# Order of the down passes, a fifth Strassen group and the spacing of the attention heads in a macaron block kernel

## The chip, the cores and the metric

The kernel runs on one core of a Trainium2 chip. The metric is the device time of one launch in microseconds (us), as the median of several runs. TensorE multiplies, VectorE and ScalarE do the elementwise work, GpSimd (POOL) and SyncE issue most of the transfers between HBM and the on-chip memory (SBUF), and TensorE writes its results to eight banks of PSUM.

## What is computed

One block on 256 frames of 2048 channels, all in float32, cut to its products:

```python
x = x + 0.5 * swiglu_ffn(rmsnorm(x), w1_gate, w1_up, w1_down)          # inner width 5632
proj = rmsnorm(x) @ w_in                                              # 2048 -> 11264
q_a, k_a, v_a, q_r, k_r, v_r, g_r, gate_a, gate_r = split(proj)
branch_a = chunked_band_attention(q_a, k_a, v_a, rel_bias) @ w_out_att  # 8 heads of 128
ret = chunkwise_retention(rotary(q_r), rotary(k_r), v_r)              # 8 heads of 128
branch_r = (silu(g_r) * ret) @ w_out_ret
x = x + (sigmoid(gate_a) * branch_a + sigmoid(gate_r) * branch_r) @ w_out
x = x + 0.5 * swiglu_ffn(rmsnorm(x), w2_gate, w2_up, w2_down)
return rmsnorm(x)
```

`swiglu_ffn` is `(silu(h @ gate) * (h @ up)) @ down`.

## The kernel before

**Products.** Every weight element is used once, so the weights stream through the chip (459.50 MB are read). A float32 weight chunk of 256 x 512 is split into a high part (`hi`, cast by ScalarE, L121) and a remainder (`lo`, subtracted by VectorE, L122); the activations are split likewise, and `three` (L129 to L131) makes one product of three matmuls: hi times hi, lo times hi, hi times lo.

**Steps.** The whole program is a list `steps`, numbered from 0 in the order in which they run; in the tile names of the standard steps (`hi587`) the number is that of the step. A *standard* step (`standard`, L133) is one chunk of an ordinary product: 12 matmuls of 512 columns. Two ordinary blocks of 512 output columns can instead be made together by `Strassen` (L479) in 28 steps of 6 matmuls, in four phases: phases 0 to 2 take four pairs of steps each (one step on a loaded quarter of the weights, one on a sum of quarters) and phase 3 takes four steps. The sums cost VectorE more than the split: in phase 0 each pair has one addition beside its two splits (L494), in phase 1 each pair has two (L549 and L536), in phases 2 and 3 there is none.

**Weaving.** `weave` (L634) places standard steps between the pairs of the Strassen groups, at a rate of standard steps per pair that it spreads by the table `SHARE`, heaviest in phase 1. A standard step waits in the queue until the blocks it needs are at hand (`job.needs`, `at_hand`, L645). In both feed-forward stages (`ffn`, L674) two of the eleven blocks (9 and 10, `PLAIN`) are ordinary; the other nine are Strassen groups that pair a block's gate and up. The standard steps are those of the plain blocks and of the passes of down: `PASSES` says which two inner blocks each pass of four column blocks takes.

**Run.** `run` (L220) goes through the steps. At step c it first prepares weights up to step c + 3 (`prep_upto`: ScalarE's cast and VectorE's remainder; there are four buffers, so that the cast of step c + 3 waits until the products of step c - 1 are through), then runs the functions that are due at c (`later`, `at`), then issues the products of step c, and, where a block ends there, its `done`.

**The middle.** First comes the woven part: four Strassen groups of the merge gates and the standard blocks of q, k and v of the attention (steps 372 to 531). Then standard steps alone: v and the gate of the retention (`nat_done` with Silu for the gate), its q and k with the rotation by `cos` and `sin` (`ret_qk_done`, L800, twelve VectorE instructions of 128 x 256), the output products of both branches. Beside these run, as functions that are due at a step, the attention (`attention`, L840: scores, transposes, values, two steps apart; heads four steps apart from eight steps after `mixed`, the first step behind the woven part) and the retention (L897).

**Side banks.** Scores, transposes and values of the heads, and every small transpose (`transpose4`, L345), take a PSUM tile by `side_tile` (L90), of which there are two: a third tile waits until the readers of one of the two before it are done. Each engine works through its instructions in the order in which they are written; nothing is reordered by a planner.

Of the kernel before, what the change touches and what calls it, by code (L numbers as in the profile page):

```python
# [8 lines left out]
F32 = mybir.dt.float32  # L9
F32R = mybir.dt.float32r  # L10
AF = mybir.ActivationFunctionType
# [4 lines left out]
P = 128  # L16
SEQ = 256
NT = SEQ // P
D = 2048
# [7 lines left out]
NB = 512  # L27
# [12 lines left out]
MIX_LEAD = 8  # L40
# [1 line left out]

SHARE = (0.85,) * 4 + (1.0,) * 4 + (0.8,) + (0.4,) * 3 + (0.15,) * 4
PLAIN = (9, 10)
PASSES = ((9, 0), (10, 1), (2, 3), (4, 5), (6,), (7,), (8,))
WARM = (6, 3)
TAIL_PARTS = ((0, slice(0, NB)), (1, slice(0, NB // 2)), (1, slice(NB // 2, NB)))

# [22 lines left out]
def block_kernel(ctx: ExitStack, tc: tile.TileContext, x, g1, w1g, w1u, w1d, gm, w_in, rel, woa, wor, wo,  # L71
                 g2, w2g, w2u, w2d, gf, cos, sin, decay, ident, out):
    nc = tc.nc
# [8 lines left out]
    dram = ctx.enter_context(tc.tile_pool(name="dram", bufs=1, space=bass.MemoryType.DRAM))  # L82

    def act_tile(dt, name):
        return apool.tile([P, 4, SEQ], dt, tag="act", name=name)
# [7 lines left out]
    def tmp_tile(name, tag="t", bufs=None):  # L93
        return tmp.tile([P, NB], F32, tag=tag, name=name, bufs=bufs)
# [9 lines left out]
    def later(n, fn):  # L104
        due.setdefault(state["step"] + n, []).append(fn)
# [87 lines left out]
    def add(jobs):  # L193
        for job in jobs:
            for k in range(0, job.nk, KC):
                steps.append(standard(job, k))
# [558 lines left out]
    nm = Norm("nm", gains[:, 1, :], True)  # L755
# [11 lines left out]
    QA, KA, VA, QR, KR, VR, GR, GA, GG = 0, W, 2 * W, 3 * W, 4 * W, 5 * W, 6 * W, 7 * W, 7 * W + D  # L767
    scale = HD ** -0.5
    tposed, nat = {}, {}
# [56 lines left out]
    def nat_done(key, b, func, after=None):  # L826
        def done(acc):
            dst = act_tile(F32, f"{key}{b}")
            nat[key, b] = dst.rearrange("p a q -> p (a q)").rearrange("p (t n) -> p t n", t=NT)
            for t in range(NT):  # L830
                nc.scalar.activation(nat[key, b][:, t, :], acc[t], func, scale=nm.scale(t))
            if after is not None:
                after()

        return done
# [56 lines left out]
    def all_attention():  # L892
        for h in range(HEADS):
            for s, stage in enumerate(attention(h)):
                later(2 + 4 * h + 2 * s, stage)

    def retention(b):  # L897
        outs = {}
# [53 lines left out]
    def proj(col, done, tags=("acc", "z")):  # L952
        return Gemm(w_in0, 0, col, D // P, nm, done, tags)


    gate_dram = [
        [dram.tile([P, NT, NB], F32, name=f"sig{key}{b}") for key in "ar"] for b in range(D // NB)
    ]

    def merge_gates(b):  # L960
        def evict(t, side, r):
            if side == 1:
                nc.scalar.activation(r, r, AF.Sigmoid)
            else:
                bank, r = r, tmp_tile(f"sg{b}{t}", "gate", 2)
                nc.scalar.activation(r, bank, AF.Sigmoid, scale=nm.scale(t))
            nc.scalar.dma_start(gate_dram[b][side][:, t, :], r)

        return Strassen(nm, w_in0, GA + b * NB, w_in0, GG + b * NB, evict)

    both = ("acc", "acc")
    weave(
        [proj(QA + b * NB, att_qk_done("qa", b), both) for b in range(2)]
        + [proj(KA + b * NB, att_qk_done("ka", b), both) for b in range(2)]
        + [proj(VA + b * NB, nat_done("va", b, AF.Copy), both) for b in range(2)],
        0, {b: (lambda b=b: merge_gates(b)) for b in range(D // NB)}, MIX_LEAD,
    )
    mixed = len(steps)
    add([proj(VR + b * NB, nat_done("vr", b, AF.Copy)) for b in range(2)])
    add([proj(GR + b * NB, nat_done("gr", b, AF.Silu)) for b in range(2)])  # L980
    for b in range(2):
        add([proj(QR + b * NB, ret_qk_done("qr", b)), proj(KR + b * NB, ret_qk_done("kr", b, lambda b=b: retention(b)))])

    merged = Operand("mg", D // NB)
    merges, of_ret = [], []
    for b in range(D // NB):
        sig = {}

        def load_sig(b=b, sig=sig):
            for i, key in enumerate("ar"):  # L990
                t = act_tile(F32, f"sig{key}{b}").rearrange("p a q -> p (a q)")
                sig[key] = t.rearrange("p (t n) -> p t n", t=NT)
                nc.gpsimd.dma_start(sig[key], gate_dram[b][i])

        def branch_a_done(acc, sig=sig):
            for t in range(NT):
                nc.vector.tensor_mul(sig["a"][:, t, :], acc[t], sig["a"][:, t, :])

        def branch_r_done(acc, sig=sig, b=b):
            for t in range(NT):  # L1000
                nc.vector.tensor_mul(sig["r"][:, t, :], acc[t], sig["r"][:, t, :])
                nc.vector.tensor_add(sig["r"][:, t, :], sig["r"][:, t, :], sig["a"][:, t, :])
            later(2, lambda: [merged.put(b, t, sig["r"][:, t, :]) for t in range(NT)])

        merges.append((len(steps), load_sig))
        add([Gemm(woa[0], 0, b * NB, W // P, att, branch_a_done)])
        of_ret.append(Gemm(wor[0], 0, b * NB, W // P, ret, branch_r_done))
# [52 lines left out]
    def at(step, fn):  # L1060
        due.setdefault(step, []).append(fn)
# [52 lines left out]
    at(mixed, set_bias)  # L1114
    at(mixed + 8, all_attention)
    at(mixed + 8, lambda: later(8, load_gain(g2, 2)))
    at(mixed + 20, set_decay)
    for step, fn in merges:
        at(step - 8, fn)
# [64 lines left out]
```

## Time and profile before

| | us |
|---|---|
| median of 3 runs (2104.57 to 2106.90) | 2105.74 |
| the profiled execution | 2106.03 |
| its span, first to last instruction | 2104.1 |
| TensorE busy | 2069.0 (98%) |
| VectorE busy | 1733.5 (82%) |
| ScalarE busy | 1396.6 (66%) |

Times in the rows are microseconds from the start of the span. A timeline row has the start, the duration of one instruction (or of several merged, with xN), engine, line, what is written from what, and in brackets the idle time of the engine just before it and what ended it. The duration of a TensorE row includes the pipeline, so starts are compared there. A row for a stretch ("windows") has the stretch, its length, then for each engine the busy time and the number of instructions, the granted TensorE clock as a share of 2.4 GHz, the share of the DMA engines and GB/s. PE is TensorE, PEld its weight loads, DVE VectorE, ACT ScalarE.

### The profile page before, as it was taken

Reading aid. Unit: us, or ns where it says so; the run is one execution under the profiler, and the core shown is the slowest. Engines: PE = TensorE matmul, PEld = TensorE weight load, DVE = VectorE, ACT = ScalarE, POOL = GpSimd, SP = SyncE. Lnnn points to the kernel's source line nnn. Section 1 sums busy time; section 2 is a strip of 40 time slices with the busy share of each in tenths; the row PEclk is TensorE's granted clock in tenths of the full one; section 3 lists DMA queues with packets and bytes.
Section 4 is the critical chain, followed back from the end, with each engine's and each line's share of the span. In section 5 each row is a group of like instructions: output and inputs, shape, how many; then the busy total and the mean of one; then the engine's idle time right before and its main releaser. Section 6 shows DMA issues by size and latency. Waiting matters only on the chain.

```text
span 2104.1 us, 25798 instructions
## 1 busy us (share of the span) xinstructions
PE 2069.0 (98%) x9280; PEld 1693.7 (80%) x9280; DVE 1733.5 (82%) x1799; ACT 1396.6 (66%) x1721; POOL 262.1 (12%) x308
## 2 busy tenths in 40 slices
PE   9999999999999999999999999999999999999998
PEld 7788878778888888888888888887888788788886
DVE  6998889889988798889556667568889988898986
ACT  7677657767777767766555434556776677677785
POOL 1111211121012110121000000010122102110200
PEclk9999999999999999999999999999999999999999
DMA  8767876797677777897656555575788668766873
GB/s 299 193 215 235 272 218 179 236 276 207 207 236 232 240 209 247 263 294 227 215 166 209 171 194 188 187 248 164 230 269 246 172 222 270 227 206 228 279 210 130
DMA packets 218384, 469.06 MB, mean 223 GB/s; under 512 B 14656, under 2 KB 15408, under 8 KB 218256
## 3 DMA queue, kind: packets, MB, share of 16 engines
q1 hardware_dynamic: 163552, 314.61, 44.9%
q0 software_dynamic: 52224, 148.54, 26.4%
q10 hardware_dynamic: 2480, 4.27, 0.5%
q8 instruction: 72, 1.18, 0.2%
q14 instruction: 56, 0.46, 0.1%
HBM read 459.50 MB, written 7.86 MB: 222 GB/s over the span
## 4 chain that ended last, share of the span: by engine, by line
PE 79%; DVE 9%; DMA 4%; issue 3%; ACT 3%; POOL 0%; ACTq 0%; POOLq 0%; DVEq 0%
PE acc L130 16%; PE acc L131 16%; PE acc L129 15%; DMA raw<-in_ffn_w_down_dram 3%; DVE lo L122 2%; ACT hi L121 1%; DMA z980x<-in_ffn_w_gate_dram 1%; PE z749a L129 0%; PE z672a L131 0%; PE z672a L129 0%; PE z494a L130 0%; PE z89a L131 0%; PE z749a L130 0%; PE z89a L130 0%; PE z494a L129 0%
## 5 line engine op out<-in xcount | busy, mean ns | idle before, releaser
L122 DVE TENSOR_TENSOR lo<-raw,hi 128x1024 fp32r<-128x1024 f32 (+1 forms) x417 | 506.1, 1218 | 209.0 <-ACT hi L121 207.1
L121 ACT CAST hi<-raw 128x1024 fp32r<-128x1024 f32 (+1 forms) x417 | 435.6, 1048 | 249.4 <-PE acc L131 171.9
L729 ACT ACTIVATE acc<-xall 128x512 f32<-128x512 f32 x96 | 57.5, 599 | 10.6 <-DVE f1g L696 4.6
L732 ACT ACTIVATE xall<-acc 128x512 f32<-128x512 f32 x96 | 56.4, 587 | 4.2 <-PE acc L131 3.8
L129 PE MATMUL acc<-hi,mgh 128*128 128x512 f32 x128 | 50.1, 392 | 0.0
L131 PE MATMUL acc<-hi,mgl 128*128 128x512 f32 x128 | 49.8, 389 | 0.0
L130 PE MATMUL acc<-lo,mgh 128*128 128x512 f32 x128 | 49.8, 389 | 0.0
L129 PE MATMUL acc<-hi,nma01h 128*128 128x512 f32 x112 | 45.0, 401 | 0.0
L129 PE MATMUL acc<-hi,nma00h 128*128 128x512 f32 x112 | 44.9, 400 | 0.0
L130 PE MATMUL acc<-lo,nma01h 128*128 128x512 f32 x112 | 44.0, 393 | 0.7 <-DVE lo L122 0.7
L130 PE MATMUL acc<-lo,nma00h 128*128 128x512 f32 x112 | 44.0, 393 | 0.3 <-DVE lo L122 0.3
L131 PE MATMUL acc<-hi,nma01l 128*128 128x512 f32 x112 | 43.8, 391 | 0.0
L131 PE MATMUL acc<-hi,nma00l 128*128 128x512 f32 x112 | 43.7, 390 | 0.0
L129 PE MATMUL acc<-hi,nma10h 128*128 128x512 f32 x112 | 43.7, 390 | 0.0
L131 PE MATMUL acc<-hi,nma11l 128*128 128x512 f32 x112 | 43.7, 390 | 0.0
L129 PE MATMUL acc<-hi,nma11h 128*128 128x512 f32 x112 | 43.7, 390 | 0.0
L131 PE MATMUL acc<-hi,nma10l 128*128 128x512 f32 x112 | 43.6, 389 | 0.0
L130 PE MATMUL acc<-lo,nma10h 128*128 128x512 f32 x112 | 43.6, 389 | 0.0
L130 PE MATMUL acc<-lo,nma11h 128*128 128x512 f32 x112 | 43.6, 389 | 0.0
L131 PEld LDWEIGHTS acc<-hi,mgl 128*128 128x128 f32 x128 | 24.0, 188 | 5.0
L129 PEld LDWEIGHTS acc<-hi,mgh 128*128 128x128 f32 x128 | 24.0, 188 | 4.9
L130 PEld LDWEIGHTS acc<-lo,mgh 128*128 128x128 f32 x128 | 24.0, 188 | 4.8
(5889 smaller groups left out, 6991.9 us busy)
## 6 DMA issues: line engine op xcount, KB each, us to landing
raw<-in_ffn_w_down_dram SPq DMA_DIRECT2D x176, 512.0 KB, 6.4
raw<-in_w_in_dram SPq DMA_DIRECT2D x112, 512.0 KB, 4.3
raw<-in_ffn_w_up_dram SPq DMA_DIRECT2D x32, 512.0 KB, 8.3
raw<-in_w_out_dram SPq DMA_DIRECT2D x32, 512.0 KB, 3.7
raw<-in_ffn_w_gate_dram SPq DMA_DIRECT2D x31, 512.0 KB, 5.1
raw<-in_w_out_att_dram SPq DMA_DIRECT2D x16, 512.0 KB, 4.8
raw<-in_w_out_ret_dram SPq DMA_DIRECT2D x16, 512.0 KB, 4.0
z380x<-in_w_in_dram POOLq DMA_DIRECT2D x8, 512.0 KB, 7.9
```

The lines of the kernel that those rows point to most:

```text
L121: nc.scalar.copy(hi[:, p, :], raw[:, p, :])
L122: nc.vector.tensor_sub(lo[:, p, :], raw[:, p, :], hi[:, p, :].bitcast(F32))
L129: nc.tensor.matmul(acc, ahi, whi, start=first, stop=False, **more)
L130: nc.tensor.matmul(acc, ahi, wlo, start=False, stop=False, **more)
L131: nc.tensor.matmul(acc, alo, whi, start=False, stop=last, **more)
L729: nc.scalar.activation(acc, xs[t][:, cols], AF.Copy, scale=2.0)
L732: nc.scalar.activation(xs[t][:, cols], acc, AF.Copy, scale=0.5)
```

## The change

Three things are changed.

1. The second pass of down takes the blocks (1, 2) and the third (10, 3), where it was (10, 1) and (2, 3). This holds for both feed-forward stages.
2. The two blocks of the retention's gate become a fifth Strassen group at the end of the woven part, by the same function as the merge gates; its results go to DRAM and are loaded again on GpSimd's queue. The first block of the retention's v becomes woven too. The woven part then has 48 instead of 40 standard steps for its groups, five groups instead of four, and `mixed` stands at step 568 instead of 532; between `mixed` and the output product of the attention are 40 steps instead of 64.
3. The heads of the attention start three steps apart instead of four.

```diff
-PASSES = ((9, 0), (10, 1), (2, 3), (4, 5), (6,), (7,), (8,))
+PASSES = ((9, 0), (1, 2), (10, 3), (4, 5), (6,), (7,), (8,))
...
-                later(2 + 4 * h + 2 * s, stage)
+                later(2 + 3 * h + 2 * s, stage)
...
+    merge_dram = [gates_dram(f"sig{b}") for b in range(D // NB)]
+    ret_dram = gates_dram("gr")
+
+    def gates(col1, col2, func, dsts):
...
         def evict(t, side, r):
             if side == 1:
-                nc.scalar.activation(r, r, AF.Sigmoid)
+                nc.scalar.activation(r, r, func)
             else:
-                bank, r = r, tmp_tile(f"sg{b}{t}", "gate", 2)
-                nc.scalar.activation(r, bank, AF.Sigmoid, scale=nm.scale(t))
-            nc.scalar.dma_start(gate_dram[b][side][:, t, :], r)
+                bank, r = r, tmp_tile(f"sg{col1}{t}", "gate", 2)
+                nc.scalar.activation(r, bank, func, scale=nm.scale(t))
+            nc.scalar.dma_start(dsts[side][:, t, :], r)
...
+    groups["gr"] = lambda: gates(GR, GR + NB, AF.Silu, ret_dram)
     weave(
...
-        + [proj(VA + b * NB, nat_done("va", b, AF.Copy), both) for b in range(2)],
-        0, {b: (lambda b=b: merge_gates(b)) for b in range(D // NB)}, MIX_LEAD,
+        + [proj(VA + b * NB, nat_done("va", b, AF.Copy), both) for b in range(2)]
+        + [proj(VR, nat_done("vr", 0, AF.Copy), both)],
+        0, groups, MIX_LEAD,
     )
     mixed = len(steps)
-    add([proj(VR + b * NB, nat_done("vr", b, AF.Copy)) for b in range(2)])
-    add([proj(GR + b * NB, nat_done("gr", b, AF.Silu)) for b in range(2)])
+    add([proj(VR + NB, nat_done("vr", 1, AF.Copy))])
...
+    def load_ret_gates():
+        for b in range(2):
+            nat["gr", b] = load_gates(f"gr{b}", ret_dram[b])
...
+    at(mixed + 16, load_ret_gates)
```

Three places show how the instructions move.

VectorE in the first feed-forward stage, in phase 1 of the group `z128` (its tiles end in the phase, the chunk and r or s; `f1g` is the plain block 10 after its up product). Before:

```order
L122 TENSOR_TENSOR loz12811s_2442<-z128x1_2120,hiz12811s_2441 128x1024
L536 TENSOR_TENSOR z128k1_2102<-z128x1_2120,z128k1_2102 128x1024
L696 SCALAR_TENSOR_TENSOR f1g100_1202<-acc11_0_2060,n1rstd_88,f1g100_1202 128x512
L696 SCALAR_TENSOR_TENSOR f1g101_1204<-acc11_1_2061,n1rstd_88,f1g101_1204 128x512
L122 TENSOR_TENSOR loz12813r_2466<-rawz12813r_2356,hiz12813r_2465 128x1024
L549 TENSOR_TENSOR z128x3_2189<-z128x3_2189,rawz12813r_2356 128x1024
L122 TENSOR_TENSOR loz12812s_2479<-z128x2_2156,hiz12812s_2478 128x1024
L536 TENSOR_TENSOR z128k2_2144<-z128x2_2156,z128k2_2144 128x1024
L122 TENSOR_TENSOR loz12813s_2491<-z128x3_2189,hiz12813s_2490 128x1024
L536 TENSOR_TENSOR z128k3_2171<-z128x3_2189,z128k3_2171 128x1024
```

Changed:

```order
L122 TENSOR_TENSOR lo144_2444<-raw144_2358,hi144_2443 128x1024
L696 SCALAR_TENSOR_TENSOR f1g100_1204<-acc11_0_2062,n1rstd_88,f1g100_1204 128x512
L696 SCALAR_TENSOR_TENSOR f1g101_1206<-acc11_1_2063,n1rstd_88,f1g101_1206 128x512
L122 TENSOR_TENSOR loz12811s_2468<-z128x1_2122,hiz12811s_2467 128x1024
L536 TENSOR_TENSOR z128k1_2104<-z128x1_2122,z128k1_2104 128x1024
L122 TENSOR_TENSOR loz12813r_2480<-rawz12813r_2377,hiz12813r_2479 128x1024
L549 TENSOR_TENSOR z128x3_2191<-z128x3_2191,rawz12813r_2377 128x1024
L122 TENSOR_TENSOR lo147_2493<-raw147_2390,hi147_2492 128x1024
```

Two standard steps of down, 144 and 147, now stand between the pairs; before, the first one came as step 148, behind six Strassen steps in a row.

TensorE at the transposes of the retention's rotated q (`qr0p0`, `qr0p1`: two side tiles). Before:

```order
L131 MATMUL acc67_1_9489<-hi574_9438,nma11l_5951 128x512
L348 MATMUL qr0p0_9549<-id_sb_78,qr00r_9458 128x128 x4
L348 MATMUL qr0p1_9555<-id_sb_78,qr01r_9468 128x128 x4
L129 MATMUL acc67_0_9488<-hi575_9477,nma01h_5946 128x512
L130 MATMUL acc67_0_9488<-lo575_9478,nma01h_5946 128x512
```

Changed:

```order
L131 MATMUL acc65_1_9396<-hi586_9321,nma11l_5953 128x512
L848 MATMUL as3_9461<-ka0T_7123,qa0T_6271 128x256
L849 MATMUL as3_9461<-ka0T_7123,qa0T_6271 128x128
L348 MATMUL qr0p0_9478<-id_sb_78,qr00r_9346 128x128 x4
L348 MATMUL qr0p1_9484<-id_sb_78,qr01r_9356 128x128 x4
L129 MATMUL acc65_0_9395<-hi587_9365,nma01h_5948 128x512
```

The scores of head 3 now stand in the same step, ahead of the two transposes: three side tiles in a row.

VectorE behind the rotation of the retention's first q block (its last instruction is L818 on `qr01r`). Before:

```order
L818 TENSOR_TENSOR qr01r_9468<-qr01r_9468,qr01u_9469 128x4x64
L122 TENSOR_TENSOR lo575_9478<-raw575_9343,hi575_9477 128x1024
L122 TENSOR_TENSOR lo576_9503<-raw576_9361,hi576_9502 128x1024
L122 TENSOR_TENSOR lo577_9521<-raw577_9384,hi577_9520 128x1024
L343 TENSOR_TENSOR attl1_9203<-av7_9526,atth1_9202 128x256
```

Changed:

```order
L818 TENSOR_TENSOR qr01r_9356<-qr01r_9356,qr01u_9357 128x4x64
L122 TENSOR_TENSOR lo587_9366<-raw587_9224,hi587_9365 128x1024
L856 SCALAR_TENSOR_TENSOR p2_9378<-as2_9375,bias0_9048 128x128 x3
L862 TENSOR_REDUCE m_9382<-p2_9378 128x1 x2
L863 TENSOR_SCALAR m_9382<-m_9382 128x2
L868 RECIPROCAL l_9383<-l_9383 128x2
L870 TENSOR_SCALAR p2_9378<-p2_9378,l_9383 128x256
L870 TENSOR_SCALAR p2_9378<-p2_9378,l_9383 128x128
L264 COPY gains_79<-gps2_9392 128x16
L122 TENSOR_TENSOR lo588_9410<-raw588_9242,hi588_9409 128x1024
L343 TENSOR_TENSOR attl0_9306<-av1_9415,atth0_9305 128x256
```

The reading of the scores of head 2 now stands behind the rotation; before, only the last head's values came that near.

## Rows read from the trace of the kernel before

**Rows 1.** The page: busy time, share of the span and instructions of each engine.

```profile
PE 2069.0 (98%) x9280; PEld 1693.7 (80%) x9280; DVE 1733.5 (82%) x1799; ACT 1396.6 (66%) x1721; POOL 262.1 (12%) x308
```

**Rows 2.** Windows of single Strassen groups, and of the stretch with attention and retention.

```profile
48.60:118.90 70.30, 67.82 (x297) 54.41 (x296) 63.84 (x64) 45.43 (x50) 12.17 (x14) 1.00 0.75 224
258.20:332.70 74.50, 70.64 (x306) 56.31 (x306) 64.17 (x62) 47.86 (x55) 10.74 (x12) 0.98 0.71 212
...
472.10:538.40 66.30, 66.30 (x298) 54.93 (x298) 59.93 (x56) 49.59 (x58) 10.70 (x12) 1.00 0.78 236
...
810.60:877.40 66.80, 66.48 (x298) 54.83 (x297) 59.70 (x54) 45.84 (x50) 10.73 (x12) 1.00 0.81 252
...
1010.10:1210.40 200.30, 199.55 (x947) 166.30 (x946) 119.48 (x209) 102.41 (x146) 6.28 (x10) 1.00 0.62 188
1431.50:1500.50 69.00, 67.60 (x298) 54.51 (x297) 60.01 (x57) 44.48 (x47) 10.71 (x12) 1.00 0.76 229
1639.50:1713.10 73.60, 69.30 (x305) 55.07 (x304) 64.00 (x61) 47.63 (x55) 10.71 (x12) 1.00 0.73 215
```

**Rows 3.** Timeline of TensorE in phase 1 of the group `z128`.

```profile
283.98 0.39 PE L129 MATMUL z128a<-hiz12810s,n1s6h 128*128 128x512 f32 x1
284.21 0.39 PE L130 MATMUL z128a<-loz12810s,n1s6h 128*128 128x512 f32 x1
...
287.68 1.31 PE L348 MATMUL f1a10p<-id_sb,f1g 128*128 128x128 f32 x8 [0.82 <-DVE f1g L696]
...
292.81 0.50 PE L130 MATMUL z128a<-loz12812s,n1s6h 128*128 128x512 f32 x1 [0.61 <-DVE loz12812s L122]
...
295.08 0.50 PE L130 MATMUL z128a<-loz12813s,n1s6h 128*128 128x512 f32 x1 [0.63 <-DVE loz12813s L122]
...
298.54 0.50 PE L130 MATMUL acc<-lo,f1a10h 128*128 128x512 f32 x1 [1.80 <-DVE lo L122]
```

**Rows 4.** Timeline of VectorE there.

```profile
282.34 1.22 DVE L122 TENSOR_TENSOR loz12812r<-rawz12812r,hiz12812r 128x1024 fp32r<-128x1024 f32 x1
283.48 1.22 DVE L549 TENSOR_TENSOR z128x<-z128x,rawz12812r 128x1024 f32<-128x1024 f32 x1
```

**Rows 5.** Windows behind that place, in the first and the second feed-forward stage.

```profile
299.70:302.70 3.00, 3.00 (x9) 2.37 (x8) 2.19 (x2) 0.09 (x1) 0.00 (x0) 0.52 1.10 214
...
1681.00:1684.00 3.00, 3.00 (x15) 2.48 (x14) 2.43 (x3) 1.05 (x1) 0.00 (x0) 1.00 1.09 208
```

**Rows 6.** Timeline of TensorE in group `z12`, behind four Strassen steps in a row of phase 1.

```profile
83.85 0.50 PE L130 MATMUL z12c<-loz1213r,n1s3h 128*128 128x512 f32 x1 [0.23 <-DVE loz1213r L122]
86.12 0.50 PE L130 MATMUL acc<-lo,n1a00h 128*128 128x512 f32 x1 [0.62 <-DVE lo L122]
```

**Rows 7.** Timeline of one head of the attention, TensorE and VectorE.

```profile
1090.31 0.59 PE L885 MATMUL av<-p,va 128*128 128x256 f32 x2
...
1090.96 0.60 PE L848 MATMUL as<-ka1T,qa1T 128*128 128x256 f32 x2
...
1091.63 1.23 DVE L122 TENSOR_TENSOR lo<-raw,hi 128x1024 fp32r<-128x1024 f32 x1 [1.49 <-ACT hi L121]
1092.78 0.42 DVE L343 TENSOR_TENSOR attl<-av,atth 128x256 fp32r<-128x256 f32 x1
1093.11 0.67 DVE L856 SCALAR_TENSOR_TENSOR p<-as,bias 128x128 f32<-128x128 f32 x3
1093.71 0.60 DVE L862 TENSOR_REDUCE m<-p 128x1 f32<-128x256 f32 x2
...
1095.77 0.55 DVE L870 TENSOR_SCALAR p<-p,l 128x256 f32<-128x256 f32 x2
```

**Rows 8.** Timeline of VectorE: first and last of the rotation's twelve instructions.

```profile
1135.59 0.42 DVE L815 TENSOR_TENSOR qr00r<-qr,cos_sb 128x256 f32<-128x256 f32 x1
...
1139.29 0.41 DVE L818 TENSOR_TENSOR qr01r<-qr01r,qr01u 128x256 f32<-128x256 f32 x1
```

**Rows 9.** Timeline: the third and fourth of four side tiles in one step.

```profile
1022.79 1.14 PE L325 MATMUL psb<-id_sb,biasT 128*128 128x128 f32 x8 [0.75 <-ACT bias L330]
```

More of the change, by code (lines that the diff above doesn't have):

```diff
@@ L953, in proj, with gates_dram @@
         return Gemm(w_in0, 0, col, D // P, nm, done, tags)
[L956 to L960, printed above, removed]
+    def gates_dram(name):
+        return [dram.tile([P, NT, NB], F32, name=f"{name}{i}") for i in range(2)]
+    merge_dram = [gates_dram(f"sig{b}") for b in range(D // NB)]
+    ret_dram = gates_dram("gr")
+    def gates(col1, col2, func, dsts):
         def evict(t, side, r):
             if side == 1:
-                nc.scalar.activation(r, r, AF.Sigmoid)
+                nc.scalar.activation(r, r, func)
             else:
-                bank, r = r, tmp_tile(f"sg{b}{t}", "gate", 2)
-                nc.scalar.activation(r, bank, AF.Sigmoid, scale=nm.scale(t))
-            nc.scalar.dma_start(gate_dram[b][side][:, t, :], r)
-        return Strassen(nm, w_in0, GA + b * NB, w_in0, GG + b * NB, evict)
+                bank, r = r, tmp_tile(f"sg{col1}{t}", "gate", 2)
+                nc.scalar.activation(r, bank, func, scale=nm.scale(t))
+            nc.scalar.dma_start(dsts[side][:, t, :], r)
+        return Strassen(nm, w_in0, col1, w_in0, col2, evict)
     both = ("acc", "acc")
+    groups = {
+        b: (lambda b=b: gates(GA + b * NB, GG + b * NB, AF.Sigmoid, merge_dram[b])) for b in range(D // NB)
+    }
+    groups["gr"] = lambda: gates(GR, GR + NB, AF.Silu, ret_dram)
     weave(
@@ L984, in block_kernel, with load_gates @@
     merged = Operand("mg", D // NB)
+    def load_gates(name, src):
+        t = act_tile(F32, name).rearrange("p a q -> p (a q)").rearrange("p (t n) -> p t n", t=NT)
+        nc.gpsimd.dma_start(t, src)
+        return t
+    def load_ret_gates():
+        for b in range(2):
+            nat["gr", b] = load_gates(f"gr{b}", ret_dram[b])
     merges, of_ret = [], []
@@ L990, in load_sig @@
             for i, key in enumerate("ar"):
-                t = act_tile(F32, f"sig{key}{b}").rearrange("p a q -> p (a q)")
-                sig[key] = t.rearrange("p (t n) -> p t n", t=NT)
-                nc.gpsimd.dma_start(sig[key], gate_dram[b][i])
+                sig[key] = load_gates(f"sig{key}{b}", merge_dram[b][i])
         def branch_a_done(acc, sig=sig):
```

## Prediction, made before the changed kernel was run

> **What bounds the kernel now.** I read the page first: TensorE is busy 98% of the span, VectorE 82% [rows 1], so the first question of every edit is whether TensorE gets more or less to do, and the second whether it is made to wait. The timeline of a stretch without waits gives the price of work: 512 columns start every 0.227 us (284.21 after 283.98) [rows 3], so a standard step of 12 takes 2.72 us and a Strassen step of 6 takes 1.36. Then I cut the span into windows that begin and end with a Strassen group [rows 2]. A group with ten standard steps is 288 matmuls of 512 columns, 65.3 us at that price. The window of the second gate group is 66.8, of a quiet feed-forward group 66.3, of the first one with a plain block inside 70.3 and 69.0. Two windows stand out: the group `z128` takes 74.5 in the first feed-forward stage and its twin 73.6 in the second. The stretch with attention and retention, in contrast, is busy 199.55 us of 200.3 [rows 2]: there nothing waits today, and VectorE is at 60%.
>
> **Change of down, part one of the sum: -9.5 us.** The timeline shows what is wrong in `z128`: TensorE waits 0.82, 0.61, 0.63 and 1.80 us, each time for VectorE [rows 3]. VectorE's instructions follow each other every 1.14 us [rows 4]; a Strassen step of phase 1 has two of them, 2.28 us for 1.36 us of matmuls. Six such steps in a row leave VectorE 5.5 us behind, more than its lead of about three steps. A standard step pays 2.72 - 1.14 = 1.58 us back. The change puts one after every second step, as everywhere else, so the 1.80 and the two waits of 0.6 lose their cause; and `f1g`, which ends the 0.82, comes one instruction (1.14 us) earlier on VectorE. In the first stage there is more: behind the 1.80 the granted clock was 0.52 for 3.0 us, that is the lower level of 1.2 GHz, and 9 matmuls took the time of 15; in the second stage the clock stayed at 1.00 at the same place [rows 5]. What is late next: the two `f1g` and the two halves of block 10's remainder stay on VectorE inside the same phase, so this group will not become as quiet as 66.3. It will resemble the other group with a plain block inside, which takes 70.3 and 69.0 [rows 2], but has four Strassen steps in a row, which this one no longer has. I take 69.3 for both: 74.5 - 69.3 + 73.6 - 69.3 = 9.5. Bounds: 67.1 for each (the quiet group and 0.8 for eight transposes more) gives 13.9; 71.1 (the worse of the two and the same 0.8) gives 5.9. The passes move only which block they read; steps from 166 on keep their place in the stage, and the transfers are as many as before.
>
> **Fifth group, part two: -1.8 us.** Two standard blocks are 192 matmuls, a group 168: 24 x 0.227 = 5.4 us less on TensorE. Against it stand 12 more splits and 12 sums, 24 x 1.14 = 27.4 us on VectorE, which has the time over the whole stretch: a gate group has 59.70 us busy of 66.8 [rows 2]. But the rate of standard steps falls from 1 to 0.96 per weighted pair, and here and there four Strassen steps stand in a row where there were two. Two of these runs lie in phase 1; the same kind shows 0.23 and 0.62 us of waits in `z12` [rows 6]. The lower bound of the cost is nothing, as in the feed-forward group of 66.3 us; the upper is five groups at 69.0 in place of 66.8, 11 us. I take 0.7 per group, 3.6 in all, nearer to the quiet groups, because only two of the five have a run in phase 1. 3.6 - 5.4 = -1.8. The four stores of the new gates and their two loads cost TensorE nothing: the loads are issued at step 584 and read at step 604, about 60 us later; on GpSimd's queue only the decay table stands behind them, four steps later, and it is read at step 596. The Silu of the gate moves from a bare stretch to the woven one on ScalarE, which is busy 45.84 of 66.8 us there.
>
> **Heads three apart, part three: +11.5 us.** TensorE's work for the heads stays. What changes is who meets whom. The stretch behind `mixed` shrinks from 64 to 40 steps, so that heads now run while the retention's q and k blocks end, and both need the two side banks and VectorE. First the row for one head: TensorE reaches the step at T = 1090.31; VectorE begins that step's remainder only at 1091.63, since the cast before it waits for a buffer; the values' remainder comes at T + 2.47, the reading of the scores takes 0.60, and p is done 3.2 us after that reading began (1096.32 against 1093.11) [rows 7]. On TensorE the values take 0.65 us, the scores as much, a transposed half block of q or k 0.44 (its four starts). With these I go through the places where the order puts a third side tile before a reader is through:
> - Step 587 (scores, then both halves of q): the second half wants TensorE at T + 1.1 and waits for the reading of the scores, T + 2.47 + 0.60 = 3.07: 2.0 us.
> - Step 585 (values of head 1 take the bank of head 2's scores): the rotation of q occupies VectorE for 4.1 us (1135.59 to 1139.29 and 0.41) [rows 8]. It begins 0.3 us before step 584 does, then come the remainder (1.14) and the reading (0.60): T + 5.5. TensorE is there at 0.6 + 0.2 + 2.72 = 3.5: 1.9 us.
> - Step 594 (values, both halves of k): the rotation of k, two remainders, head 5's whole chain of 3.2, a remainder and 0.33 stand ahead on VectorE, to T + 10.9 counted from step 592; TensorE is there at 7.7: 3.2 us.
> - Step 601 (transposes of head 7): head 7's chain, then the rotation, a remainder and 0.33 end 11.2 us after step 599 began, TensorE is there after 7.9: 3.3 us.
> - Step 603 (values, both halves of q again): the bank waits only for a copy: 1.1 us, between [rows 9] and the first place.
>
> The sum is 11.5 us. No cover is left for it, since a wait of TensorE is lost for good. The only case of this kind in the trace, four side tiles in one step, shows 0.75 us [rows 9]; there the reader is one copy of ScalarE and no rotation is ahead. Three waits of that size, 2.3 us, are the lower bound. The upper is 11.5 and the clock lost behind each of the five, 8 us more. I take my own count, since each of its terms has a row, and add half of one loss of clock (0.8), because [rows 5] show one in two.
>
> **Sum.** 2106.0 (the profiled execution) - 9.5 - 1.8 + 11.5 + 0.8 = 2107.0. The median lies 0.3 below the profiled execution: 2106.7.
>
> **Rivals.** (a) *The bank waits stay small.* In the trace no rotation makes TensorE wait: the window is busy 199.55 of 200.3 us [rows 2]. If the new meetings cost 0.75 each, three of them, the time is 2106.0 - 9.5 - 1.8 + 2.3 - 0.3 = 2096.7. Against it: before, no rotation has two head stages behind it within two steps, and now three have. (b) *VectorE becomes the bound of the woven gate part.* At 0.96 standard steps per pair five groups take 69.0 us instead of 67.5, 7.5 us more: 2114.2. It decides as soon as waits for a remainder pass 0.7 us per group on the mean. For it: phase 1 alone leaves VectorE behind by 1.9 us per pair. Against it: 59.70 of 66.8 us [rows 2]. (c) *The clock falls behind every wait of the attention.* One loss costs 1.6 us (8 matmuls at twice 0.2), five cost 8.0 instead of 0.8: 2113.9. The row for it is the 0.52 of the first stage, the row against it the 1.00 of the second [rows 5]. The Trainium skill has a rule for this ("TensorE: Matmul & The Clock Gate", Part 1: The HAM clock gate): the throttled state is the default and activity releases it, so an idle TensorE falls back to half the clock. [...] (d) *The waits of down only move*, to the third pass or to phase 2 behind: without part one the time is 2116.2. That the change doesn't do what it says is excluded: the order shows the standard steps between the pairs and 24 fewer matmuls.
>
> **How the numbers follow.** The forecast has 0.55, (a) 0.20, (b) 0.10, (c) 0.10, (d) 0.05. A measurement of this kernel can tell about 0.2%, 4.2 us, from no change. The forecast's own spread is some 4 us to each side, from the bounds of part one and part three, so a tenth of it lies outside of 0.2%, mostly above. Faster is (a) and a little of the forecast, 0.22; slower is (b), (c), (d) and a little, 0.28; the same 0.50. The range reaches from (a) to (b) and (c): 2096.5 to 2114.5, which leaves out some of (a) below and (d) above. The forecast alone would have 2102 to 2111.
>
> **What would show it.** Right: windows of about 69 us for the group `z128` and its twin, with no run of waits for VectorE in phase 1; gate groups between 66.3 and 68; and in the stretch behind the gates five waits of TensorE of 1 to 3.5 us, before values, before the transposes of head 7 and before the second halves of q, k and q. Wrong would be: waits there below 1 us each (a), waits for remainders spread over the gate groups (b), a granted clock near 0.5 behind the waits (c), or the `z128` window still above 72 (d).

## The result, and the profile after

The changed kernel takes 2116.0 us (median of 6 runs, 2113.7 to 2118.4) against 2105.15 (2103.9 to 2106.9) for the kernel before: a ratio of 1.0050, with a 95% interval of 1.0037 to 1.0063. It became slower by 10.9 us. The forecast was 2106.7, no change, and the range ended at 2114.5. The profiled execution has a span of 2114.5 us, 10.4 more than the one of before.

The page hardly shows it: TensorE's busy time is the same within 1.1 us, its share of the span still 98% (compare [rows 1]).

```profile
span 2114.5 us, 25819 instructions
PE 2070.1 (98%) x9256; PEld 1691.4 (80%) x9256; DVE 1761.4 (83%) x1825; ACT 1407.0 (67%) x1734; POOL 273.5 (13%) x322
```

The windows show where it is. These are, in the changed kernel, the group `z128`, its twin in the second feed-forward stage (the group `z800` by its new number), the woven part with its five groups, and the stretch behind it from step 576 to step 608 with the eight heads, three rotations and the first half of the retention. The columns are the window, its length, busy time and instructions of PE, PEld, DVE, ACT and POOL, granted clock, DMA share and GB/s.

```profile
258.90:329.80 70.90, 68.89 (x306) 55.33 (x305) 64.36 (x62) 47.54 (x55) 10.72 (x12) 1.00 0.72 223
1651.80:1722.60 70.80, 68.81 (x305) 55.10 (x304) 64.17 (x62) 47.51 (x55) 10.73 (x12) 1.00 0.72 223
...
738.20:1069.30 331.10, 327.94 (x1449) 268.00 (x1448) 294.92 (x266) 229.71 (x248) 49.77 (x55) 1.00 0.77 242
1093.90:1221.60 127.70, 116.32 (x547) 96.11 (x546) 77.72 (x174) 55.47 (x96) 6.27 (x10) 0.96 0.46 151
```

The two windows of down fell from 74.5 and 73.6 [rows 2] to 70.9 and 70.8: 6.4 us gained. From the first gate group to the end of the attention the kernel before needs 467.7 us (742.70 to 1210.40), the changed one 483.4 (738.20 to 1221.60): 15.7 lost. With 6.4 gained and 15.7 lost the span should grow by 9.3 us; it grew by 10.4, and the other 1.1 us, spread over other groups, were not traced. So the change gains where it was meant to, and loses it in the last of the four windows: TensorE is idle for 11.4 of 127.7 us, and the granted clock is 0.96; before, the heads and the retention stood in a stretch of which 199.55 of 200.3 us were busy, at 1.00 [rows 2].

The timeline of TensorE names the waits; in brackets stands the idle time before an instruction and what ended it.

```profile
1123.98 0.67 PE L885 MATMUL av<-p,va 128*128 128x256 f32 x2 [1.59 <-DVE p L856]
...
1133.85 1.09 PE L348 MATMUL qr0p<-id_sb,qr01r 128*128 128x128 f32 x4 [2.04 <-DVE p L856]
...
1135.16 0.63 PE L130 MATMUL acc<-lo,nma01h 128*128 128x512 f32 x1
1135.59 0.63 PE L131 MATMUL acc<-hi,nma01l 128*128 128x512 f32 x1
...
1159.59 0.63 PE L348 MATMUL kr0p<-id_sb,kr00r 128*128 128x128 f32 x4 [0.34 <-DVE p L856]
1163.77 0.66 PE L348 MATMUL kr0p<-id_sb,kr01r 128*128 128x128 f32 x4 [3.55 <-DVE attl L343]
...
1194.88 0.57 PE L877 MATMUL apt<-id_sb,p 128*128 128x128 f32 x3 [3.02 <-DVE attl L343]
...
1205.78 0.66 PE L348 MATMUL qr1p<-id_sb,qr11r 128*128 128x128 f32 x4 [0.85 <-ACT qr1T L783]
```

These are the five places of the forecast, in order: step 585 (values), 587 (second half of q), 594 (both halves of k), 601 (transposes of head 7), 603 (second half of the second q). They sum to 1.59 + 2.04 + 3.89 + 3.02 + 0.85 = 11.4 us; the forecast had 11.5. The two rows of 512 columns show something more: they start 0.43 us apart, not 0.227 [rows 3]. Windows of 3 us behind the first, the second, the fourth and the fifth of those rows with a bracket give the granted clock (the column ahead of the last two):

```profile
1123.98:1126.98 3.00, 3.00 (x14) 2.55 (x15) 1.77 (x8) 2.19 (x6) 0.00 (x0) 1.00 0.55 175
1133.85:1136.85 3.00, 3.00 (x9) 2.54 (x10) 1.86 (x7) 1.45 (x5) 0.00 (x0) 0.50 0.56 180
1163.77:1166.77 3.00, 3.00 (x11) 2.47 (x12) 0.69 (x1) 0.00 (x0) 0.00 (x0) 0.63 0.66 209
1194.88:1197.88 3.00, 3.00 (x10) 2.42 (x11) 1.61 (x3) 0.48 (x1) 0.00 (x0) 0.57 0.56 185
```

Behind three of the five waits TensorE ran at the lower level, 1.2 GHz, for a while; the 3 us that follow the wait of 2.04 us lie at it throughout.

The longest wait can be followed on VectorE. Its timeline ahead of 1163.77, first and last of the rotation of k, and what stands behind it:

```profile
1152.47 0.42 DVE L815 TENSOR_TENSOR kr00r<-kr,cos_sb 128x256 f32<-128x256 f32 x1
...
1156.16 0.42 DVE L818 TENSOR_TENSOR kr01r<-kr01r,kr01u 128x256 f32<-128x256 f32 x1
1156.50 2.35 DVE L122 TENSOR_TENSOR lo<-raw,hi 128x1024 fp32r<-128x1024 f32 x2
1158.77 0.68 DVE L856 SCALAR_TENSOR_TENSOR p<-as,bias 128x128 f32<-128x128 f32 x3
...
1162.15 1.23 DVE L122 TENSOR_TENSOR lo<-raw,hi 128x1024 fp32r<-128x1024 f32 x1 [0.19 <-ACT hi L121]
1163.30 0.42 DVE L343 TENSOR_TENSOR attl<-av,atth 128x256 fp32r<-128x256 f32 x1
```

The transposes of k need the bank of `av`. Its reader `attl` is a short instruction, but the rotation, two remainders, the whole chain of head 5 and a third remainder stand ahead of it, 10.8 us from 1152.47 to 1163.30.

### The profile page after: what moved, and what is told of

Read it like the earlier page. It is cut to its first block, busy times and chain, and to the rows that moved or that the text cites. A ratio compares the mean times of both kernels' runs of the same rounds, so it can differ in the third digit from the quotient of the medians.

```text
span 2114.5 us, 25819 instructions
## 1 busy us (share of the span) xinstructions
PE 2070.1 (98%) x9256; PEld 1691.4 (80%) x9256; DVE 1761.4 (83%) x1825; ACT 1407.0 (67%) x1734; POOL 273.5 (13%) x322
## 5 line engine op out<-in xcount | busy, mean ns | idle before, releaser
L122 DVE TENSOR_TENSOR lo<-raw,hi 128x1024 fp32r<-128x1024 f32 (+1 forms) x401 | 487.2, 1219 | 180.7 <-ACT hi L121 179.1
L121 ACT CAST hi<-raw 128x1024 fp32r<-128x1024 f32 (+1 forms) x401 | 418.7, 1047 | 222.1 <-PE acc L131 135.9
L729 ACT ACTIVATE acc<-xall 128x512 f32<-128x512 f32 x96 | 57.5, 599 | 8.4 <-DVE f2g L696 3.5
L129 PE MATMUL acc<-hi,nma01h 128*128 128x512 f32 x96 | 39.4, 411 | 0.0
L131 PE MATMUL acc<-hi,nma00l 128*128 128x512 f32 x96 | 38.0, 396 | 0.0
L129 PE MATMUL acc<-hi,nma11h 128*128 128x512 f32 x96 | 37.7, 393 | 0.0
L129 PE MATMUL acc<-hi,nma10h 128*128 128x512 f32 x96 | 37.7, 393 | 0.0
L131 PE MATMUL acc<-hi,nma11l 128*128 128x512 f32 x96 | 37.6, 392 | 0.0
L130 PE MATMUL acc<-lo,nma10h 128*128 128x512 f32 x96 | 37.6, 392 | 0.0
L130 PE MATMUL acc<-lo,nma11h 128*128 128x512 f32 x96 | 37.6, 392 | 0.0
L131 PE MATMUL acc<-hi,nma10l 128*128 128x512 f32 x96 | 37.4, 390 | 0.0
```

Source lines behind the costliest of these rows:

```text
L121: nc.scalar.copy(hi[:, p, :], raw[:, p, :])
L122: nc.vector.tensor_sub(lo[:, p, :], raw[:, p, :], hi[:, p, :].bitcast(F32))
L129: nc.tensor.matmul(acc, ahi, whi, start=first, stop=False, **more)
L130: nc.tensor.matmul(acc, ahi, wlo, start=False, stop=False, **more)
L131: nc.tensor.matmul(acc, alo, whi, start=False, stop=last, **more)
L729: nc.scalar.activation(acc, xs[t][:, cols], AF.Copy, scale=2.0)
```

## Experiments

Theory after the result: (1) the loss is made where heads and rotations meet at the two side banks; (2) about 11 us of it are the waits themselves, the rest is the clock that falls behind them; (3) down's order gives some 6 us by itself, not 9.5. Rivals: the spacing of three is too dense in itself; two banks are too few whatever VectorE does; the slow matmuls behind the waits have another cause than the clock.

### Down's order alone

```
 (the kernel before)
-PASSES = ((9, 0), (10, 1), (2, 3), (4, 5), (6,), (7,), (8,))
+PASSES = ((9, 0), (1, 2), (10, 3), (4, 5), (6,), (7,), (8,))
```

> The kernel before with the new order of down's passes alone. Theory 1 (what the changed kernel's windows show): the group z128 takes 70.9 us and its twin 70.8, so 74.5 - 70.9 + 73.6 - 70.8 = 6.4 us are gained: 2098.8. Theory 2 (the forecast's part one, with the rest of the difference caused by the other two parts): both windows at 69.3, 9.5 us gained: 2095.6.

Measured: 2098.6 us, ratio 0.9967 (0.9954 to 0.9979), 6.6 us gained. The windows are those of the changed kernel within 0.1 us:

```profile
258.20:329.00 70.80, 68.85 (x305) 55.24 (x304) 64.26 (x62) 47.69 (x55) 10.73 (x12) 1.00 0.73 223
1635.60:1706.30 70.70, 68.75 (x305) 55.20 (x304) 64.17 (x62) 47.60 (x55) 10.70 (x12) 1.00 0.74 223
```

Theory 1 holds: part one is a gain on its own, a third smaller than forecast, and the rest of the change more than undoes it.

### Without the rotation

```
-                s = tmp_tile(f"{key}{b}{t}", "gate", 2)
-                nc.scalar.activation(s, acc[t], AF.Copy, scale=nm.scale(t))
                 r = tmp_tile(f"{key}{b}{t}r", "qk", 4)
-                (views of s, r, u and of the angles; six VectorE instructions)
+                nc.scalar.activation(r, acc[t], AF.Copy, scale=nm.scale(t))
                 srcs.append(r)
```

> The changed kernel without the rotation of the retention's q and k: ScalarE writes the scaled block straight into the tile that is transposed; the 12 instructions of 0.33 us per block on VectorE are left out, and so is the rotation in what is computed. Theory 1 (three of the five waits are the rotation's burst on VectorE, ahead of the readers of a side bank; two are the bank alone): step 585 from 1.59 to 0, step 601 from 3.02 to 0, step 594 from 3.9 to about 1.4; step 587 stays at 2.0 and step 603 at 0.8; together 4.2 instead of 11.4, and one or two falls of the clock instead of three: 2116.0 - 7.2 - 2.5 = about 2106. Theory 2 (two side banks are too few, whatever stands on VectorE): the five waits stay within 0.5 us each: 2115 to 2116.

Measured: 2107.1 us, ratio 1.0011 (1.0003 to 1.0020). The waits of TensorE in the stretch (total, times, longest; behind the place of the edit the line numbers are 12 lower, so L844 is the L856 of the changed kernel):

```profile
PE kr0p L348 <- DVE attl L343: 2.8, 1, 2.8
PE qr0p L348 <- DVE p L844: 2.0, 1, 2.0
PE qr1p L348 <- ACT qr1T L783: 0.9, 1, 0.9
PE apt L865 <- DVE attl L343: 0.4, 1, 0.4
```

The values of step 585 wait no more, the transposes of head 7 wait 0.4 instead of 3.0. Step 587 keeps its 2.0 to the hundredth: there the bank alone is the cause, with no rotation ahead, as the forecast had counted it. Step 594 keeps 2.8 of 3.9, more than the 1.4 expected. VectorE shows why: even without the rotation it comes late to the chain of head 5, since it waits for ScalarE's cast of the remainder ahead of it, and the reader of the bank stands behind that chain.

```profile
1156.63 1.23 DVE L122 TENSOR_TENSOR lo<-raw,hi 128x1024 fp32r<-128x1024 f32 x1 [1.33 <-ACT hi L121]
...
1162.30 0.42 DVE L343 TENSOR_TENSOR attl<-av,atth 128x256 fp32r<-128x256 f32 x1
```

The stretch is 119.0 us, 8.7 shorter; the waits give 5.3 of it, and the rest goes with two of the three falls of the clock. So without the rotation about half of the loss stays, at the two banks. The halves can't be added up as causes, though: the next version but one keeps the rotation and loses nothing there.

### TensorE kept at work in the waits

```
+FILLS = {("av", 1): 5, ("qr", 0): 7, ("kr", 0): 13, ("apt", 7): 11}
+    def fill(n):
+        spare = acc_tile("fill", "z")
+        hi, wide = nm.form("a00", 0)[0], nm.pair("a00")[0][:, 0:4, :]
+        for i in range(n):
+            nc.tensor.matmul(spare, hi, wide, start=True, stop=True)
 (called ahead of these values and transposes, and between the halves of q and k)
```

> The changed kernel with TensorE kept at work while it would wait: 5 matmuls of 512 columns into a spare bank ahead of the values of step 585, 7 ahead of the second half of q at step 587, 13 ahead of that of k at step 594, 11 ahead of the transposes of step 601: 36 x 0.227 = 8.2 us of matmuls inside 10.2 us of waits. Theory 1 (the 6 us beyond the direct waits are the clock that falls behind three of them): the granted clock stays at 1.00 in this stretch, the stretch gets 5 to 6 us shorter although TensorE does more: 2110 to 2111. Theory 2 (these 6 us are not the clock's; small instructions and VectorE are slower there for another reason): no gain, 2116, or up to 1 us more where a filling overruns its wait.

Measured: 2110.2 us, ratio 1.0021 (1.0012 to 1.0030), 5.9 us faster than the changed kernel with 36 matmuls more. The windows of the whole stretch and behind the last three of the same four places:

```profile
1092.20:1215.30 123.10, 119.85 (x583) 99.12 (x582) 77.81 (x174) 55.49 (x96) 6.27 (x10) 1.00 0.51 157
...
1132.16:1135.16 3.00, 3.00 (x15) 2.54 (x16) 1.86 (x7) 1.46 (x5) 0.00 (x0) 1.00 0.59 182
1160.63:1163.63 3.00, 3.00 (x15) 2.56 (x16) 0.69 (x1) 0.00 (x0) 0.00 (x0) 1.00 0.67 190
1190.15:1193.15 3.00, 3.00 (x15) 2.54 (x16) 1.61 (x3) 0.48 (x1) 0.00 (x0) 1.00 0.60 193
```

The waits are together as long as before: 36 x 0.227 = 8.2 us are filled, and 3.3 us are left of them. But the clock stays at 1.00 and the stretch is 127.7 - 123.1 = 4.6 us shorter. That is the price of the clock, measured by itself. It is not an accident of the one trace: the mean granted clock of the whole run was 0.998 or 0.999 in all eleven runs with the waits filled, and 0.995 to 0.997 in all six of the changed kernel. The medians lie 5.9 us apart; the 1.3 us beyond the 4.6 were not traced. The Trainium skill ("TensorE: Matmul & The Clock Gate", Part 1: The HAM clock gate) says that activity is what releases the throttle; this run agrees, since the clock did not fall once matmuls stood where TensorE had been idle.

### Heads apart from the rotations

```
-                later(2 + 3 * h + 2 * s, stage)
+                later(2 + 4 * h + 2 * s, stage)
-    at(mixed + 8, all_attention)
+    at(mixed + 4, all_attention)
-            to_transposed(key, b, srcs, 4 if after is None else 3)
+            to_transposed(key, b, srcs, 6 if key + str(b) == "qr1" else 4)
-                later(5 + 2 * i + 2 * s, stage)
-        later(5 + 2 * 4, finish)
+                later(6 + 2 * i + 2 * s, stage)
+        later(6 + 2 * 4, finish)
```

> The changed kernel with its heads four steps apart again but begun four steps earlier (scores at mixed + 6, + 10, ...), so that heads use the side banks at even steps only; the transposes of q and k at odd steps (k one step later, the second q two steps later), and the retention's first four heads one step later, at odd steps. Theory 1 (the cost lies in the meetings, not in the shorter stretch): no wait of TensorE above 1 us and clock 1.00 behind the gates; what stays is the gain of down's order and of the fifth group: 2105.2 - 6.3 - 1.5 = 2097.4, up to 2099.5 with small waits. Theory 2 (eight heads and four rotations in 40 steps are too much for VectorE wherever they stand): waits of 5 us or more stay, 2103 or above.

Measured: 2099.2 us, ratio 0.9969 (0.9956 to 0.9981), 16.8 us faster than the changed kernel, with the same matmuls and the same VectorE work. The stretch from step 576 to 608:

```profile
1098.70:1208.00 109.30, 109.30 (x541) 91.67 (x539) 74.99 (x164) 52.72 (x90) 6.27 (x10) 1.00 0.56 176
```

TensorE is busy for all of it. Eight heads and the rotations fit into the shorter stretch, if no third side tile is asked for close behind a head or a rotation. The edit moves three things at once, the heads, the transposes of q and k and the retention's heads; which of them could have stayed in place was not tried, except for the spacing alone, which comes next.

### Four steps apart, begun where the changed kernel begins

```
-                later(2 + 3 * h + 2 * s, stage)
+                later(2 + 4 * h + 2 * s, stage)
```

> The changed kernel with its heads four steps apart again, begun at the same step as in the changed kernel; everything else stays. Theory 1 (the cost is made where a third side tile is asked for within a step or two of a rotation or of a head, so the spacing alone moves the meetings): step 587 has no wait now, but step 594 has values, scores and both halves of k, some 3 us, and steps 598 and 602 have values, scores and a head of the retention, some 1.5 us each; with one or two falls of the clock 2105 to 2110. Theory 2 (the spacing of three is the cause by itself): all of the loss goes, 2098 to 2099.

Measured: 2105.65 us, ratio 1.0004 (0.9995 to 1.0013). The waits move to where theory 1 puts them, with lesser sizes:

```profile
PE rs L908 <- DVE attl L343: 1.6, 2, 0.8
PE kr0p L348 <- DVE attl L343: 1.5, 1, 1.5
PE apt L877 <- DVE retl L343: 1.1, 1, 1.1
PE kr1p L348 <- ACT kr1T L783: 0.8, 1, 0.8
PE retp L348 <- DVE attl L343: 0.6, 1, 0.6
```

None is above 1.5 us, and the granted clock is 1.00 in the stretch; the falls that theory 1 allowed for did not come. The distance of the heads by itself is not what matters: four apart costs less than three apart here and more than four apart from an earlier step.

This version is the change without its third part, so the runs give the price of each part when they are added one after the other: down's order 2105.15 to 2098.6, a gain of 6.6 us; the fifth group, with the heads where they then stand, to 2105.65, a loss of 7.1; the spacing of three, to 2116.0, a loss of 10.4.

### Three steps apart in the kernel before

```
 (the kernel before)
-                later(2 + 4 * h + 2 * s, stage)
+                later(2 + 3 * h + 2 * s, stage)
```

> The kernel before with its heads three steps apart, nothing else: there the heads end at step 567, before the first rotation, which follows step 571. Theory 1 (a head every three steps costs nothing as long as no rotation and no transposes of q or k fall among the heads): no wait above 1 us in that stretch, 2105.2, within 1 us. Theory 2 (three apart is too dense for VectorE or the two side banks in itself): waits of 0.5 us and more at each head, 2109 or above.

Measured: 2105.2 us, ratio 1.0002 (0.9993 to 1.0011). The stretch that was 200.3 us [rows 2] is 200.3 again, with the one wait of `psb` [rows 9] that it had:

```profile
1010.00:1210.30 200.30, 199.55 (x947) 166.30 (x946) 119.39 (x209) 101.14 (x145) 6.26 (x10) 1.00 0.61 188
```

So part three, the line that looks like the cause, costs nothing where the stretch is 64 steps long. It is part two that pulls the rotations 24 steps nearer (40 steps in place of 64), and heads and rotations then meet; there the same line costs 10.4 us.

### The fifth group, with the heads apart

The version with the heads apart from the rotations, with `PASSES` as in the kernel before.

> The version with the heads apart from the rotations, with the order of down's passes of the kernel before: what is left against the kernel before is the fifth group and the new place of the heads. Theory 1 (the fifth group is worth 24 matmuls, 5.4 us, less the waits for VectorE that it brings into the woven part, 3.9 us in the trace of the changed kernel, and the heads cost nothing): 1 to 2 us gained, 2103.5 to 2104.5, which the runs alone can hardly tell from no change; the stretch from the first gate group to the end of the attention takes about 467 us, against 467.7 before. Theory 2 (it costs nothing on VectorE): 2099.8.

Measured: 2104.0 us, ratio 0.9993 (0.9984 to 1.0003): 1.0 us, which the runs cannot tell from none. The trace has it at 465.9 us from the first gate group to the end of the attention, against 467.7 before:

```profile
743.60:1209.50 465.90, 462.01 (x2105) 380.08 (x2104) 384.00 (x450) 297.51 (x358) 58.26 (x69) 1.00 0.74 230
```

These 1.8 us are what the forecast gave this part, but in two other traces with the heads apart, with down's new order, the stretch is 467.3 and 466.7: the gain is 0.4 to 1.8 us by the trace that one takes. Nor do its terms come out. TensorE's busy time falls by 4.0 us (465.98 to 462.01), not by 5.4, and its waits grow by 2.2 (1.7 to 3.9), not by 3.6; the two misses cancel. The runs agree that the gain is small: with down's new order the version with the fifth group and the heads apart is 0.7 us slower than down's order alone (2099.2 against 2098.6), and with the later seed of the next section it is 2.1 faster (2096.2 against 2098.3).

### The second seed of a down block one step later

What keeps `z128` at 70.9 us? In the changed kernel ScalarE waits 3.5 us with the seed of the next down block (L729 writes the bank, which the last reader `f1g` still holds), and the cast that VectorE needs next stands behind it. First ScalarE, then VectorE, then TensorE:

```profile
287.13 0.60 ACT L729 ACTIVATE acc<-xall 128x512 f32<-128x512 f32 x1 [3.52 <-DVE f1g L696]
```

```profile
288.73 1.23 DVE L122 TENSOR_TENSOR loz12811s<-z128x,hiz12811s 128x1024 fp32r<-128x1024 f32 x1 [0.97 <-ACT hiz12811s L121]
```

```profile
294.55 0.50 PE L130 MATMUL acc<-lo,f1a1h 128*128 128x512 f32 x1 [0.40 <-DVE lo L122]
...
301.43 0.50 PE L130 MATMUL acc<-lo,f1a2h 128*128 128x512 f32 x1 [0.60 <-DVE lo L122]
```

VectorE loses 0.97 us, and TensorE waits for it a few steps later. The same wait of ScalarE stood in the trace of the kernel before, where the forecast could have read it:

```profile
287.66 0.60 ACT L729 ACTIVATE acc<-xall 128x512 f32<-128x512 f32 x1 [4.60 <-DVE f1g L696]
```

The edit, in `close`:

```
-        if follow is not None:
+        if follow is not None and job.evict is None:
+            later(1, lambda: begin(1))
+        elif follow is not None:
             begin(1)
```

> The kernel before with the new order of down's passes and the second seed of a down block (ScalarE's write into the bank that the block adds to) put one step later when it follows an up block, so that it no longer stands on ScalarE ahead of the next cast while it waits for VectorE's f1g. Theory 1 (what is left in the group z128 beyond the forecast 69.3 us is this: ScalarE waits 3.5 us at 287.1, VectorE 0.97 us for the cast behind it, and TensorE later 0.40, 0.23 and 0.60 us for VectorE): the idle 0.97 of VectorE goes, the windows of 70.9 and 70.8 fall to 69.5 to 70, 2096.4. Theory 2 (VectorE has too much work in phase 1 in any case): the windows stay at 70.8, 2098.6.

> The version with the heads apart from the rotations, and the later second seed as well: the candidate for the fastest. Theory 1: both gains add, 2099.2 - 2.2 = 2097.0. Theory 2: the seed gives nothing, 2099.2.

Measured: 2098.3 us with down's order alone, ratio 0.9967 (0.9955 to 0.9980), no difference that the runs can tell from 2098.6; and 2096.2 us with the heads apart, ratio 0.9957 (0.9944 to 0.9969), 3.0 below the version without it, in another set of runs. The runs thus leave it open; the traces show what the edit does. In the second of the two kernels VectorE has no idle time ahead of that remainder,

```profile
286.70 1.22 DVE L122 TENSOR_TENSOR loz12811s<-z128x,hiz12811s 128x1024 fp32r<-128x1024 f32 x1
```

and the windows of `z128` and its twin are

```profile
257.90:327.60 69.70, 68.31 (x305) 55.35 (x304) 64.06 (x62) 47.99 (x55) 10.72 (x12) 1.00 0.74 226
1633.00:1702.70 69.70, 68.30 (x306) 55.33 (x305) 64.05 (x62) 47.96 (x55) 10.73 (x12) 1.00 0.74 226
```

1.1 us less each. With down's order alone they are 69.7 and 70.3, so that the twin gains 0.4 there. Of TensorE's three waits the 0.40 and the 0.23 are gone and the 0.60 is still there; the other half of the 1.1 us is shorter busy time (68.85 to 68.31), which was not followed. By these windows the seed is 0.4 to 1.1 of the 1.5 us that the forecast missed per window. The last kernel, 2096.2 us, is faster than both: 9 us below the kernel before and 20 below the changed one.

### The rotation on GpSimd

```
-                    nc.vector.tensor_mul(r4[:, :, j, :], s4[:, :, j, :], c)
+                    nc.gpsimd.tensor_mul(r4[:, :, j, :], s4[:, :, j, :], c)
 (and the five others of a half in the same way)
```

> The changed kernel with the rotation of the retention's q and k on GpSimd in place of VectorE. Theory 1 (the burst costs where it stands in VectorE's order, and GpSimd, which has little to do there, is through with it before the transposes, 8 to 11 us later): as without the rotation, 2107, with the waits at step 587 and 594 left. Theory 2 (GpSimd needs more than those 8 to 11 us for a block, so that the transposes wait for it, or it slows VectorE meanwhile): 2114 or above, with waits of the transposes of q and k for GpSimd.

Measured: 2117.8 us, ratio 1.0062 (1.0050 to 1.0075). Theory 2 holds. Two of the waits of TensorE, the longest:

```profile
PE kr1p L348 <- POOL kr11r L818: 4.4, 1, 4.4
PE kr0p L348 <- DVE attl L343: 4.3, 1, 4.3
```

The values of step 585 wait 0.3 and head 7's transposes 0.9, nearly as little as without the rotation (none and 0.4). But the last block of k takes GpSimd from 1214.72 to 1226.0, 11.3 us, and its transposes come three steps after the block's end. Three of its instructions, and VectorE's beside them:

```profile
1216.83 0.73 POOL L816 TENSOR_TENSOR kr10u<-kr,sin_sb 128x256 f32<-128x256 f32 x1
1217.53 1.72 POOL L817 TENSOR_TENSOR kr10r<-kr10r,kr10u 128x256 f32<-128x256 f32 x1
1219.21 1.74 POOL L818 TENSOR_TENSOR kr10r<-kr10r,kr10u 128x256 f32<-128x256 f32 x1
```

```profile
1216.97 1.67 DVE L122 TENSOR_TENSOR lo<-raw,hi 128x1024 fp32r<-128x1024 f32 x1 [1.11 <-ACT hi L121]
1219.12 1.23 DVE L122 TENSOR_TENSOR lo<-raw,hi 128x1024 fp32r<-128x1024 f32 x1 [0.48 <-ACT hi L121]
```

Where a remainder of VectorE runs, an instruction of GpSimd of the same shape takes 1.72 us in place of 0.73. VectorE's remainder takes 1.67 where an instruction of GpSimd had begun before it (1216.83), and its usual 1.23 where it began first (1219.12).

## Why the prediction was wrong

- **The five bank waits (11.5 us): right in place and size, four of five in cause.** 2.0, 1.9, 3.2, 3.3 and 1.1 were forecast; 2.04, 1.59, 3.89, 3.02 and 0.85 measured. The run without the rotation shows that the split into "bank alone" (step 587) and "rotation ahead" (585, 601) was right too. At step 594 the size was luck: the forecast's end of T + 10.9 holds 4.1 us of rotation, and without it TensorE, there at 7.7, should not have waited at all. 2.8 us stay. The count let VectorE run without a gap, but it waits for casts ahead of head 5's chain.
- **The clock (0.8 us): this term failed.** It was 4.6 us, measured by the filled waits. The row used showed a fall behind one wait in two [rows 5]; it was applied once, to one of the waits, though there were five. Applied to each it would have been 2.5 falls of 1.6 us, 4.0 us, and the forecast 2109.9, at the edge of what the prediction calls slower. Rival (c) had the mechanism and priced it at 8.0 us for five falls; three fell, at about 1.5 us each.
- **Part one (9.5 us): the second term that failed.** It was 6.4 us. The stalls it named went (the 1.80, the 0.61 and 0.63 and the 0.82 have no successor above 0.8). The window that it took for both, 69.3 us, came from another group with a plain block inside; but there no down block follows with its seed into a bank that VectorE still reads. The measured 70.9 lies within the bounds given, 67.1 to 71.1, at the upper end. ScalarE's wait for that bank is 0.4 to 1.1 of the missing 1.5 us per window; the rest stays open.
- **Part two (-1.8 us): the sum fits, partly by luck.** With the heads apart it is 0.4 to 1.8 us, and its two terms, 5.4 saved and 3.6 paid, were 4.0 and 2.2. VectorE did not become the bound of the woven part: rival (b) falls. The shorter stretch behind it, which part two makes, was counted under part three.
- **What remains.** The 15.7 us lost up to the end of the attention and the 0.4 to 1.8 that part two gains there make 16.1 to 17.5 us for the meetings; 11.4 are waits and 4.6 the clock. The 0.1 to 1.5 us left, and 1.1 us spread over other groups, were not traced to a cause.

Summed up: 3.1 us of part one, 3.8 of the clock and up to 2.6 of the rest make at most 9.5; between forecast and result lie 9.3. Rival (a), small waits, falls in the changed kernel, and rival (d) falls with the 6.6 us that down's order gains alone.

## What to carry to other kernels

A gain in TensorE's work can bring two clumps of side work together that shared nothing before: after such an edit, list for each step how many tiles of the smallest PSUM pool are asked for, and what stands on the in-order engine ahead of each reader. A forecast of TensorE waits is half a forecast; each wait wants a term of its own for the clock that may fall behind it, here about 1.5 us a fall (4.6 us for three). And a wait on an engine that is only in the middle of a chain (ScalarE's seed here) is worth looking for wherever the next engine has no slack.

## What the runs showed of the hardware

How often the clock falls is less regular than a single pair of rows suggests. Waits of TensorE in these traces, with the granted clock of the 3 us behind each:

| Wait, us | Kernel and place | Clock behind it |
|---|---|---|
| 1.47 | heads four apart, first k | 1.00 |
| 1.59 | changed, step 585 | 1.00 |
| 1.68 to 1.70 | all twelve kernels, first feed-forward stage, 39 us from the start | 1.00 in all |
| 1.80 | before, first and second stage [rows 3] | 0.71 and 1.00 |
| 1.83, 1.79 | fifth group with the heads apart, the same two places | 0.64 and 1.00 |
| 1.80, 1.81 | before with heads three apart, the same two places | 1.00 and 1.00 |
| 2.04 | changed, without rotation, rotation on GpSimd: step 587 | 0.50, 0.59 and 1.00 |
| 2.82 | without rotation, step 594 | 1.00 |
| 3.02, 3.55 | changed, steps 601 and 594 | 0.57 and 0.63 |
| 4.32, 4.43 | rotation on GpSimd, step 594 and last k | 0.61 and 0.50 |

Behind the same wait of 2.04 us at the same place the clock fell in two kernels and not in the third. It fell behind all of the four longest, behind four of the ten between 1.79 and 2.9 us, and behind none of the shorter ones. No length can be read from these rows that decides. The clock differs between runs of one kernel too: without the rotation the two runs with a mean clock of 0.996 took 2110.8 and 2111.1 us, the one with 0.999 took 2106.9.

The rotation's instructions on 128x256 floats start 0.70 us apart on GpSimd, against 0.34 on VectorE [rows 8], and in the rows above one takes 1.0 us more when a remainder of VectorE, with both its operands in SBUF, runs beside it. The Trainium skill ("SBUF — State Buffer", Terms) says that the two engines share one pair of ports, locked for a whole instruction, so that the loser blocks. The rows above agree with that: VectorE's 1.67 us are its usual 1.23 and about what was left of GpSimd's instruction when it began (1216.97 to 1217.56), and GpSimd's 1.72 us from 1217.53 are its usual 0.73 and about what was then left of VectorE's (until 1218.64).
